# Stick-breaking attention of a streaming encoder layer: heads taken in pairs, the TensorE order written out

## The chip, the cores and the metric

One core of a Trainium2 chip runs the whole kernel in one launch. The metric is the time of one execution on the device in microseconds; the median of several runs is quoted. "The profile" is one execution taken by the hardware profiler, "the trace" its instructions.

## The reference

One layer of a hybrid encoder, for a prompt of 512 tokens and eight samples of 16 tokens each (640 token rows together), model width 1024, all in float32. After a norm, one wide input projection feeds three token mixers (stick-breaking attention, a pooling mixer, gated linear attention), whose outputs are gated, merged and projected; cross-attention into 256 memory tokens and a gated feed-forward block follow. The change is in the stick-breaking attention (6 heads of 64 channels):

```
z = einsum('bqhd,bkhd->bhqk', q, k) * 64 ** -0.5
mask = k_pos < q_pos
log_beta = log_sigmoid(z)
log_fail = where(mask, log_sigmoid(-z), 0)
after = cumsum(log_fail, axis=3, reverse=True) - log_fail
w = where(mask, exp(log_beta + after), 0)
out = einsum('bhqk,bkhd->bqhd', w, v)
```

Prompt queries see the prompt's own keys. Each sample's 16 queries see 256 cached keys and the sample's own 16.

## The kernel before

All weights are split into a high and a low part, and every large product is three matmuls per tile of 128 (`products`, L114). Weights arrive on SP's DMA queue in a ring of buffers (`raw`, three; `wh` and `wl`, four each): `load_raw` (L73), then a cast on ScalarE (L83) and a subtraction on VectorE (L89). The part of the input projection that is kept by rows comes in seven column blocks, n0 to n6, of five units each, one per 128 token rows (`nat_unit`); a unit is 24 matmuls into a PSUM bank with the tag g, and a ScalarE copy. Blocks 0 and 1 are done first. `proj_nat(2)` to `proj_nat(4)` stand in the program behind the attention, blocks 5 and 6 in the next stage (gated linear attention).

PSUM has eight banks, two for each of the tags g, t, z and o (`bank`, L63).

**Order.** Instructions are written as a plain program. The framework orders each engine's instructions by priority (place in the program) among those whose inputs and buffers are free, so work that stands later may run earlier. Inside `tc.manual_schedule(engines={PE})` TensorE's instructions keep the written order.

**What comes ahead of the attention.** Queries and keys are projected with channels on partitions into `qkT` (tiles 0 to 2 queries, 3 to 5 keys; of each tile, head 2p lies in rows 0 to 63, head 2p+1 in rows 64 to 127). Then five key blocks are transposed back (`tp_k`, L460), copied into `kst` (two buffers, L462) and stored (L464, L467). The pool `poolw`, which holds `kst` and the pooling mixer's tiles, is released, and the attention's pool `sbw` opens in its place.

**Attention.** A prompt unit is one query block i of 128 rows and one to three heads; with i + 1 key blocks its scores are at most 512 columns wide. `sb_prompt_a` makes the scores (`z`, L508, one head's 64 rows of the array), then `softplus` (Abs, Exp, Ln on ScalarE, L476 to L478; one VectorE instruction, L479), a mask on the diagonal block on GpSimd (L217), and `stick`: a scan from the right on VectorE (L487), `z` minus the scan (L488), Exp on ScalarE (L489), and a mask again. `sb_prompt_b` transposes the weights block by block (`tp_w`, L521), copies them out (L523) and, once both heads of a pair are there, multiplies with the values (`po`, L534, the two heads into the two halves of the output's partitions). A sample unit is a pair of heads and four samples: cached keys and values are loaded (`kn`, L544; `vn`, L548; one buffer each), keys are transposed (`tp_kc`, L555) and copied into `kt` (L556, L557), scores of four samples go to four groups of 32 output rows (`zs`, L567), then the same steps, 272 columns wide; `sb_sample_b` transposes (L582, L583), multiplies (`pos`, L587, L591), copies (L593), transposes back (L595) and splits. There are 18 prompt units (12 of one head with i = 3 and 2, 4 with i = 1, 2 of three heads with i = 0) and six sample units, one behind every three prompt units; `sb_..._b` of a unit stands two units behind its `sb_..._a`.

Of the kernel before, what the change touches and what calls it, by code (L numbers as in the profile page):

```python
# [16 lines left out]
P = 128  # L17
# [16 lines left out]
def tile_hybrid_stream_step(  # L34
# [466 lines left out]
    def sb_prompt_a(i, hs):  # L501

        n = (i + 1) * P
        m = len(hs)
        z = bank([P, 512], "z", "z")[:, 0:m * n]
        for j, h in enumerate(hs):
            p_, r = h // 2, slice((h % 2) * 64, (h % 2) * 64 + 64)
            nc.tensor.matmul(z[:, j * n:(j + 1) * n], qkT[r, p_, i * P:(i + 1) * P], qkT[r, 3 + p_, 0:n],  # L508
                             start=True, stop=True)
        t = softplus(z, m * n)  # L510
        mask_diag(t, i, m, n)
        w = stick(z, t, m, n)
        mask_diag(w, i, m, n)
        return w

    def sb_prompt_b(i, hs, w):
        n = (i + 1) * P
        m = len(hs)
        tp = bank([P, 512], "t", "tp_w")
        for k in range(m * (i + 1)):  # L520
            nc.tensor.transpose(tp[:, k * P:(k + 1) * P], w[:, k * P:(k + 1) * P], ident)  # L521
        wT = sbw.tile([P, 512], F32, tag="wT", bufs=2, name="wT")
        nc.vector.tensor_copy(wT[:, 0:m * n], tp[:, 0:m * n])  # L523
        for j, h in enumerate(hs):
            wTs[i, h] = wT[:, j * n:(j + 1) * n]
        if hs[0] == 0:
            oacc[i] = bank([P, 3, P], "o", "po")
        for h in hs:
            if h % 2 == 0:
                continue  # L530
            p_ = h // 2
            for k in range(i + 1):
                for r in range(2):
                    nc.tensor.matmul(oacc[i][64 * r:64 * r + 64, p_, :], va[:, k, (2 * p_ + r) * 64:(2 * p_ + r + 1) * 64],  # L534
                                     wTs[i, 2 * p_ + r][:, k * P:(k + 1) * P], start=(k == 0), stop=(k == i))
            if h == 5:
                split(oa_h[:, :, i * P:(i + 1) * P], oa_l[:, :, i * P:(i + 1) * P], oacc[i])

    def sb_sample_a(p_, g):
        kn = sbw.tile([P, 4, 2, P], F32, tag="kn", bufs=1, name="kn")  # L540
        vn = sbw.tile([P, 4, 2, P], F32, tag="vn", bufs=1, name="vn")
        for j in range(4):
            b = 4 * g + j
            nc.sync.dma_start(kn[:, j], cache_sb_k[0, b, :, 2 * p_:2 * p_ + 2, :]  # L544
                              .rearrange("(t p) h d -> p t (h d)", p=P))
        for j in range(4):
            b = 4 * g + j
            nc.sync.dma_start(vn[:, j], cache_sb_v[0, b, :, 2 * p_:2 * p_ + 2, :]  # L548
                              .rearrange("(t p) h d -> p t (h d)", p=P))
        kt = sbw.tile([P, 4, 272], F32, tag="kt", bufs=1, name="kt")  # L550
        for half in range(2):
            tp = bank([P, 2, 2, P], "t", "tp_kc")
            for j in range(2):
                for t_ in range(2):
                    nc.tensor.transpose(tp[:, j, t_, :], kn[:, 2 * half + j, t_, :], ident)  # L555
            nc.any.tensor_copy(kt[:, 2 * half:2 * half + 2, 0:256], tp.rearrange("p j t k -> p j (t k)"))  # L556
        nc.gpsimd.tensor_copy(kt[:, :, 256:272],  # L557
                              qkT[:, 3 + p_, 512 + 64 * g:576 + 64 * g].rearrange("p (j q) -> p j q", q=16))
        bdq = sbw.tile([P, 4, 32], F32, tag="bdq", bufs=2, name="bdq")
        nc.gpsimd.memset(bdq, 0.0)  # L560
        for r in range(2):
            rs = slice(64 * r, 64 * r + 64)
            nc.gpsimd.tensor_copy(bdq[rs, :, 16 * r:16 * r + 16],
                                  qkT[rs, p_, 512 + 64 * g:576 + 64 * g].rearrange("p (j q) -> p j q", q=16))
        z = bank([P, 272], "z", "zs")
        for j in range(4):
            nc.tensor.matmul(z[32 * j:32 * j + 32, :], bdq[:, j, :], kt[:, j, :],  # L567
                             start=True, stop=True)
        t = softplus(z, 272)
        nc.vector.tensor_tensor(t[:, 256:272], t[:, 256:272], smask, ALU.mult)  # L570
        w = stick(z, t, 1, 272)
        nc.vector.copy_predicated(w[:, 256:272], invm.bitcast(U32), zero16)
        we = sbw.tile([P, NB, 16], F32, tag="we", bufs=2, name="we")
        nc.vector.tensor_tensor(we, w[:, None, 256:272].broadcast_to([P, NB, 16]),
                                gmask[:, g, :, None].broadcast_to([P, NB, 16]), ALU.mult)
        return vn, w, we

    def sb_sample_b(p_, g, st):
        vn, w, we = st
        tp = bank([P, 3, P], "t", "tp_ws")  # L580
        for k in range(2):
            nc.tensor.transpose(tp[:, k, :], w[:, k * P:(k + 1) * P], ident)  # L582
        nc.tensor.transpose(tp[:, 2, :], we.rearrange("p b k -> p (b k)"), ident)  # L583
        wT = sbw.tile([P, 3, P], F32, tag="wT", bufs=2, name="wTs")
        nc.any.tensor_copy(wT, tp)
        po = bank([P, P], "o", "pos")
        nc.tensor.matmul(po, wT[:, 2, :], va[:, 4, p_ * P:(p_ + 1) * P], start=True, stop=False)  # L587
        for k in range(2):
            for j in range(4):
                js = slice(32 * j, 32 * j + 32)  # L590
                nc.tensor.matmul(po[js, :], wT[:, k, js], vn[:, j, k, :], start=False, stop=(k == 1))  # L591
        on = sbw.tile([P, P], F32, tag="on", bufs=1, name="on")
        nc.vector.tensor_copy(on, po)  # L593
        po = bank([P, P], "t", "tp_on")
        nc.tensor.transpose(po, on, ident)  # L595
        pv = po.rearrange("p (j r q) -> p j r q", r=2, q=16)
        for r in range(2):
            rs = slice(64 * r, 64 * r + 64)
            cs = slice(512 + 64 * g, 576 + 64 * g)
            split(oa_h[rs, p_, cs].rearrange("p (j q) -> p j q", q=16),  # L600
                  oa_l[rs, p_, cs].rearrange("p (j q) -> p j q", q=16), pv[rs, :, r, :])
# [4 lines left out]
    nc.gpsimd.memset(zero16, 0.0)  # L606

    up = [(3, (h,)) for h in range(6)] + [(2, (h,)) for h in range(6)]
    up += [(1, (0, 2)), (1, (1, 3)), (1, (4,)), (1, (5,)), (0, (0, 2, 4)), (0, (1, 3, 5))]
    us = [(p_, g) for p_ in range(3) for g in range(2)]  # L610
    units = []
    for j, u in enumerate(up):
        units.append((sb_prompt_a, sb_prompt_b, u))
        if j % 3 == 2 or j >= 17:
            if us:
                units.append((sb_sample_a, sb_sample_b, us.pop(0)))
# [869 lines left out]
```

## Time and profile before

| | |
|---|---|
| runs shown, median (lowest to highest) | 1299.34 us (1299.01 to 1300.34) |
| profiled execution, its own time | 1298.68 us |
| its span, first to last instruction | 1297.0 us |
| TensorE matmuls busy | 1275.6 us, 98% of the span |
| VectorE, ScalarE, GpSimd busy | 776.2, 596.5, 41.2 us |
| mean granted clock of TensorE | 0.997 of full speed |

The profile counts an engine as busy from an instruction's start to its end. Matmuls overlap each other, so what a matmul costs is read from start to next start. In a timeline row "x16" merges sixteen instructions, and the length runs from the first start to the last end. "z<-qkT 64x512" means that tile `z` is computed from tile `qkT`, 64 partitions by 512 elements; a float32 product of two operands appears as two matmuls, a transpose as one. A row's square bracket says how long the engine stood idle before it and what ended that. SP's queue shows when a DMA is issued, not when its data lands.

### The profile page before, as it was taken

How to read it: one execution, taken by the hardware profiler on the slowest of the kernel's cores; microseconds unless marked ns; L12 is line 12 of the kernel's file. 1: busy time of each engine (PE TensorE's matmuls, PEld its weight loads, DVE VectorE, ACT ScalarE, POOL GpSimd, SP SyncE). 2: the span in 40 equal slices, each digit the busy share in tenths (PEclk: the TensorE clock that was granted, in tenths of full speed). 3: DMA queues.
4: the chain of work that ended last, by engine and by line, in shares of the span. 5: the costliest groups of instructions: out<-in, count | busy, mean ns of one | idle time of the engine just before them, and what ended most of it. 6: DMA issues, size and time to landing. Idle time of an engine off the chain costs nothing.

```text
span 1297.0 us, 21377 instructions
## 1 busy us (share of the span) xinstructions
PE 1275.6 (98%) x8493; PEld 1156.5 (89%) x8493; DVE 776.2 (60%) x1458; ACT 596.5 (46%) x1198; POOL 41.2 (3%) x162
## 2 busy tenths in 40 slices
PE   8999999999999999999999999999999999999997
PEld 8998777988999999987998878899898989898995
DVE  7433875387478455437535434598466767675766
ACT  5324665454353445435434543476352525243452
POOL 2101111001000000000000000000000000000000
PEclk9999999999999999999999999999999999999999
DMA  7324332201321232232448860242232313132232
GB/s 239 103 78 120 94 100 66 62 1 55 82 78 32 82 122 67 72 143 69 133 178 273 299 224 1 81 147 82 65 98 76 98 54 114 49 98 82 82 123 105
DMA packets 132889, 133.88 MB, mean 103 GB/s; under 512 B 15798, under 2 KB 116741, under 8 KB 132789
## 3 DMA queue, kind: packets, MB, share of 16 engines
q1 hardware_dynamic: 132501, 132.23, 32.4%
q8 instruction: 67, 1.10, 0.3%
q0 software_dynamic: 288, 0.29, 0.1%
q14 instruction: 33, 0.27, 0.1%
HBM read 121.72 MB, written 10.77 MB: 102 GB/s over the span
## 4 chain that ended last, share of the span: by engine, by line
PE 91%; DVE 4%; ACT 2%; DMA 2%; issue 1%; SPq 0%; POOL 0%; DVEq 0%; ACTq 0%
PE ps_g L114 13%; PE fX L1237 11%; PE ps_d L114 8%; PE ps_n L114 8%; PE fZ L1237 5%; PE ps_xq L114 4%; PE ps_b L114 4%; PE acc L1308 4%; PE acc L1309 4%; PE acc L1310 3%; PE ps_qk L114 3%; PE fY L1237 3%; PE pl L721 2%; PE ps_xk L114 2%; PE ps_xv L114 1%; PE z L508 1%
## 5 line engine op out<-in xcount | busy, mean ns | idle before, releaser
L1308 PE MATMUL acc<-wh_o,ga_h 128*128 128x512 f32 (+1 forms) x224 | 87.4, 390 | 0.0
L1309 PE MATMUL acc<-wl_o,ga_h 128*128 128x512 f32 (+1 forms) x224 | 87.3, 390 | 0.0
L1310 PE MATMUL acc<-wh_o,ga_l 128*128 128x512 f32 (+1 forms) x224 | 87.2, 389 | 0.0
L816 ACT ACTIVATE sgm<-ps_g 128x320 f32<-128x320 f32 x48 | 20.9, 435 | 66.0 <-PE ps_g L114 65.9
L1310 PEld LDWEIGHTS acc<-wh_o,ga_l 128*128 128x128 f32 x224 | 42.0, 188 | 9.6
L1308 PEld LDWEIGHTS acc<-wh_o,ga_h 128*128 128x128 f32 x224 | 42.0, 188 | 9.3
L1309 PEld LDWEIGHTS acc<-wl_o,ga_h 128*128 128x128 f32 x224 | 42.1, 188 | 9.2
L1237 PE MATMUL fX<-fT_h,wl_f 128*128 128x320 f32 x160 | 49.5, 309 | 0.0
L1237 PE MATMUL fX<-fT_l,wh_f 128*128 128x320 f32 x160 | 49.4, 309 | 0.0
L1237 PE MATMUL fZ<-S_h,wl_f 128*128 128x320 f32 x160 | 49.4, 309 | 0.0
L1237 PE MATMUL fX<-fT_h,wh_f 128*128 128x320 f32 x160 | 49.4, 309 | 0.0
L1237 PE MATMUL fX<-S_h,wh_f 128*128 128x320 f32 x160 | 49.4, 309 | 0.0
L1237 PE MATMUL fX<-S_l,wh_f 128*128 128x320 f32 x160 | 49.4, 309 | 0.0
L1237 PE MATMUL fZ<-S_l,wh_f 128*128 128x320 f32 x160 | 49.4, 309 | 0.0
L1237 PE MATMUL fZ<-S_h,wh_f 128*128 128x320 f32 x160 | 49.4, 309 | 0.0
L1237 PE MATMUL fX<-S_h,wl_f 128*128 128x320 f32 x160 | 49.3, 308 | 0.0
L143 ACT CAST wh_f<-ra 128x1024 fp32r<-128x1024 f32 x20 | 21.0, 1052 | 45.9 <-PE acc L1310 26.8
L144 DVE TENSOR_TENSOR wl_f<-ta,wh_f 128x1024 fp32r<-128x1024 f32 x20 | 24.5, 1225 | 27.5 <-ACT wh_f L143 27.5
L817 DVE TENSOR_SCALAR sgm<-sgm 128x320 f32<-128x320 f32 x48 | 15.5, 325 | 40.4 <-ACT sgm L816 40.3
L143 ACT CAST wh_f<-ta 128x1024 fp32r<-128x1024 f32 x20 | 21.0, 1049 | 38.9 <-PE acc L1310 29.1
L1393 DVE TENSOR_TENSOR X<-acc,X 128x512 f32<-128x512 f32 x40 | 27.2, 690 | 17.9 <-PE acc L1310 17.9
L144 DVE TENSOR_TENSOR wl_f<-ra,wh_f 128x1024 fp32r<-128x1024 f32 x20 | 24.4, 1222 | 22.4 <-ACT wh_f L143 22.2
(1004 smaller groups left out, 4246.0 us busy)
## 6 DMA issues: line engine op xcount, KB each, us to landing
raw_o<-in_w_ffn_out_dram SPq DMA_DIRECT2D x22, 512.0 KB, 3.5
ra<-in_w_ffn_in_dram SPq DMA_DIRECT2D x40, 256.0 KB, 3.3
rb<-in_w_ffn_in_dram SPq DMA_DIRECT2D x40, 256.0 KB, 3.4
kc<-in_cache_mem_k_dram SPq DMA_DIRECT2D x16, 512.0 KB, 4.8
vc<-in_cache_mem_v_dram SPq DMA_DIRECT2D x16, 512.0 KB, 5.4
raw_mix<-in_w_mix_out_dram SPq DMA_DIRECT2D x8, 512.0 KB, 4.4
raw_xo<-in_w_xo_dram SPq DMA_DIRECT2D x8, 512.0 KB, 6.1
kn<-in_cache_sb_k_dram SPq DMA_DIRECT2D x24, 128.0 KB, 2.4
```

Of the source, the lines that this page charges most:

```text
L114: ins = nc.tensor.matmul(ps, a, b, start=(j == 0), stop=(j == len(todo) - 1))
L143: nc.scalar.copy(h, src)
L144: nc.vector.tensor_tensor(l, src, h.bitcast(F32), ALU.subtract)
L508: nc.tensor.matmul(z[:, j * n:(j + 1) * n], qkT[r, p_, i * P:(i + 1) * P], qkT[r, 3 + p_, 0:n], start=True, stop=True)
L721: nc.tensor.matmul(pl[0:nk, h], X[:, h, 0:nk], mv_, start=True, stop=True)
L816: nc.scalar.activation(s, ps, AF.Exp, scale=-1.0)
L817: nc.vector.tensor_scalar(s, s, 2.0 ** 63, None, ALU.min)
L1237: nc.tensor.matmul(ps, w_, m_, start=(start and j == 0), stop=(stop and j == 11), skip_group_check=True)
L1308: nc.tensor.matmul(ps, ah, wh[:, 0, c0:c0 + w], start=first, stop=False)
L1309: nc.tensor.matmul(ps, ah, wl[:, 0, c0:c0 + w], start=False, stop=False)
L1310: nc.tensor.matmul(ps, al, wh[:, 0, c0:c0 + w], start=False, stop=last)
L1393: nc.vector.tensor_tensor(dst, ps, dst, addop)
```

## The change

Prompt units become objects of an even and an odd head (or lists of them), sample units objects with their steps as methods, and TensorE's order over all of them and over the fifteen units of projection blocks 2 to 4 is written out. A prompt unit's `scores` issues the matmuls of the even and of the odd head in turn, into two z banks; `turn` transposes and copies the even head's weights on VectorE, the odd head's on ScalarE. There are now nine prompt units (three with i = 3, three with i = 2, two with i = 1, one with i = 0), with a sample unit behind each of the first six. A sample unit's `load` and `keys` stand right behind the scores of the sample unit before it; its output and the transpose back use g banks instead of o and t, the copies of `kt` go one to VectorE and one to ScalarE, `on` to ScalarE. In step j of the loop, TensorE does the transposes of unit j-2, the transpose back of unit j-3, one projection unit, the output of unit j-2, the scores of unit j, and the keys of the next sample unit. The first steps are the keys of sample unit 0 and the scores of prompt unit 0. `softplus`, `stick`, `mask_diag` and the sample unit's scores are the same as before. Cut to its core:

```diff
-    def sb_prompt_a(i, hs):
...
-        for j, h in enumerate(hs):
-            p_, r = h // 2, slice((h % 2) * 64, (h % 2) * 64 + 64)
-            nc.tensor.matmul(z[:, j * n:(j + 1) * n], qkT[r, p_, i * P:(i + 1) * P], qkT[r, 3 + p_, 0:n],
-                             start=True, stop=True)
...
+        def scores(self):
+            i, n = self.i, self.n
+            m = len(self.hs[0])
+            zs = [bank([P, 512], "z", "z")[:, 0:m * n] for _ in range(2)]
+            for j in range(m):
                 for r in range(2):
+                    p_, rs = self.hs[r][j] // 2, slice(64 * r, 64 * r + 64)
+                    nc.tensor.matmul(zs[r][:, j * n:(j + 1) * n], qkT[rs, p_, i * P:(i + 1) * P],
+                                     qkT[rs, 3 + p_, 0:n], start=True, stop=True)
+            self.w = []
+            for z in zs:
+                t = softplus(z, m * n)
+                mask_diag(t, i, m, n)
+                w = stick(z, t, m, n)
+                mask_diag(w, i, m, n)
+                self.w.append(w)
...
+                if r:
+                    nc.scalar.copy(wT[:, 0:len(hs) * self.n], tp[:, 0:len(hs) * self.n])
+                else:
+                    nc.vector.tensor_copy(wT[:, 0:len(hs) * self.n], tp[:, 0:len(hs) * self.n])
...
-            nc.any.tensor_copy(kt[:, 2 * half:2 * half + 2, 0:256], tp.rearrange("p j t k -> p j (t k)"))
...
+                if half:
+                    nc.scalar.copy(kt[:, 2:4, 0:256], tp.rearrange("p j t k -> p j (t k)"))
+                else:
+                    nc.vector.tensor_copy(kt[:, 0:2, 0:256], tp.rearrange("p j t k -> p j (t k)"))
...
-        po = bank([P, P], "o", "pos")
...
+            po = bank([P, P], "g", "pos")
...
-        nc.vector.tensor_copy(on, po)
-        po = bank([P, P], "t", "tp_on")
...
+            nc.scalar.copy(self.on, po)
...
-    up = [(3, (h,)) for h in range(6)] + [(2, (h,)) for h in range(6)]
-    up += [(1, (0, 2)), (1, (1, 3)), (1, (4,)), (1, (5,)), (0, (0, 2, 4)), (0, (1, 3, 5))]
...
-    for fb_, u_, st_ in pend:
-        fb_(*u_, st_)
-    for c in range(2, 5):
-        proj_nat(c)
+    pu = [PromptUnit(i, (h,), (h + 1,)) for i in (3, 2) for h in (0, 2, 4)]
+    pu += [PromptUnit(1, (0, 2), (1, 3)), PromptUnit(1, (4,), (5,)), PromptUnit(0, (0, 2, 4), (1, 3, 5))]
+    su = [SampleUnit(p_, g) for p_ in range(3) for g in range(2)]
     units = []
+    for j in range(len(pu)):
+        units.append(pu[j])
+        if j < len(su):
+            units.append(su[j])
+    fill = [(c, i) for c in range(2, 5) for i in range(NT)]
+    ws = {}
+    su[0].load()
+    with tc.manual_schedule(engines={mybir.EngineType.PE}):
+        su[0].keys()
+        units[0].scores()
+        for j in range(1, len(units) + 2):
+            old = units[j - 2] if 2 <= j else None
+            if old:
+                old.turn()
+            if 3 <= j and isinstance(units[j - 3], SampleUnit):
+                units[j - 3].back()
+            if fill:
+                c, i = fill.pop(0)
+                if i == 0:
+                    ws[c] = load_nat(c)
+                nat_unit(c, ws[c], i)
+            if old:
+                old.out()
+            if j < len(units):
+                units[j].scores()
+                if isinstance(units[j], SampleUnit):
+                    k = su.index(units[j]) + 1
+                    if k < len(su):
+                        su[k].load()
+                        su[k].keys()
```

## Rows read from the trace of the kernel before

**Rows 1.** The page: busy time by engine.
```profile
PE 1275.6 (98%) x8493; PEld 1156.5 (89%) x8493; DVE 776.2 (60%) x1458; ACT 596.5 (46%) x1198; POOL 41.2 (3%) x162
```

**Rows 2.** Busy time by stretch of attention: us, then PE, PEld, DVE, ACT, POOL, clock, DMA.
```profile
107.38:124.41 17.03, 16.97 (x121) 15.06 (x120) 6.37 (x9) 6.77 (x16) 2.83 (x9) 1.00 0.65 187
124.41:217.06 92.65, 91.54 (x684) 66.33 (x685) 69.96 (x137) 61.55 (x138) 15.92 (x52) 1.00 0.29 82
```

**Rows 3.** Timeline of two heads that start together: ScalarE, VectorE, GpSimd.
```profile
117.33 1.09 ACT L476 ACTIVATE sp<-z 128x512 f32<-128x512 f32 x2
...
120.00 1.29 DVE L479 SCALAR_TENSOR_TENSOR sp<-z,sp 128x512 f32<-128x512 f32 x2 [10.55 <-ACT sp L478]
121.21 2.56 DVE L487 TENSOR_TENSOR_SCAN w<-sp 128x512 f32<-128x512 f32 x2
123.69 1.26 DVE L488 TENSOR_TENSOR w<-z,w 128x512 f32<-128x512 f32 x2
...
125.68 0.29 POOL L217 TENSOR_SCALAR_AFFINE_SELECT w<-w 128x128 f32<-128x128 f32 x1 [0.31 <-ACT w L489]
```

**Rows 4.** Timeline of TensorE: first matmul of projection block 5.
```profile
217.06 0.29 PE L114 MATMUL ps_n<-wh_n5a,hT_h 128*128 128x278 f32 x1
```

**Rows 5.** Timeline of TensorE in attention: start, length (us), line, tile, how many.
```profile
107.38 1.12 PE L508 MATMUL z<-qkT 64*128 64x512 f32 x2
108.43 0.87 PE L460 MATMUL tp_k<-ident,qkT 128*128 128x128 f32 x6
...
116.84 0.29 PE L114 MATMUL ps_n<-wh_n2a,hT_h 128*128 128x276 f32 x1
...
119.89 0.29 PE L114 MATMUL ps_n<-wh_n2a,hT_h 128*128 128x276 f32 x1
...
139.24 0.49 PE L587 MATMUL pos<-va,wTs 128*128 128x128 f32 x2
139.66 0.65 PE L591 MATMUL pos<-vn,wTs 128*32 128x128 f32 x16
140.24 0.40 PE L114 MATMUL ps_n<-wl_n3a,hT_h 128*128 128x276 f32 x1
...
147.09 1.14 PE L567 MATMUL zs<-kt,bdq 128*32 128x272 f32 x8
148.16 0.65 PE L521 MATMUL tp_w<-ident,w 128*128 128x128 f32 x4
148.74 0.91 PE L508 MATMUL z<-qkT 64*128 64x384 f32 x2
149.58 0.66 PE L521 MATMUL tp_w<-ident,w 128*128 128x128 f32 x4
...
151.61 1.09 PE L534 MATMUL po<-wT,va 128*64 128x128 f32 x14
152.63 0.40 PE L114 MATMUL ps_n<-wh_n3a,hT_h 128*128 128x276 f32 x1
...
189.01 0.70 PE L508 MATMUL z<-qkT 64*128 64x256 f32 x2
```

**Rows 6.** Timeline of SP's queue (issues), and how long the key loads take.
```profile
111.38 1.10 SPq L464 DMA_DIRECT2D out_dram<-kst  x2
116.99 0.33 SPq L467 DMA_DIRECT2D out_dram<-kst  x1
117.80 1.98 SPq L544 DMA_DIRECT2D kn<-in_cache_sb_k_dram  x4
...
DMA to landing us min/median/max: 2.0/2.4/3.6
```

**Rows 7.** The same table of stretches, near the kernel's start.
```profile
10.00:11.00 1.00, 0.00 (x0) 0.00 (x0) 1.00 (x3) 0.00 (x0) 0.00 (x0) 1.00 1.00 325
11.00:12.00 1.00, 0.91 (x5) 0.94 (x6) 1.00 (x2) 0.00 (x0) 0.00 (x0) 0.75 1.17 282
...
14.00:15.00 1.00, 1.00 (x7) 1.00 (x6) 0.93 (x3) 1.00 (x1) 0.00 (x0) 0.55 1.17 339
```

More of the change, by code (lines that the diff above doesn't have):

```diff
@@ L499, in mask_diag @@
             sel(d, [[0, m], [-1, P]], 0, 1, ALU.is_gt)
-    def sb_prompt_a(i, hs):
-        n = (i + 1) * P
-        m = len(hs)
-        z = bank([P, 512], "z", "z")[:, 0:m * n]
-        for j, h in enumerate(hs):
-            p_, r = h // 2, slice((h % 2) * 64, (h % 2) * 64 + 64)
-            nc.tensor.matmul(z[:, j * n:(j + 1) * n], qkT[r, p_, i * P:(i + 1) * P], qkT[r, 3 + p_, 0:n],
-                             start=True, stop=True)
[L510 to L532, printed above, removed]
-                for r in range(2):
-                    nc.tensor.matmul(oacc[i][64 * r:64 * r + 64, p_, :], va[:, k, (2 * p_ + r) * 64:(2 * p_ + r + 1) * 64],
-                                     wTs[i, 2 * p_ + r][:, k * P:(k + 1) * P], start=(k == 0), stop=(k == i))
-            if h == 5:
-                split(oa_h[:, :, i * P:(i + 1) * P], oa_l[:, :, i * P:(i + 1) * P], oacc[i])
@@ L539, in sb_sample_a @@
[L539 to L555, printed above, removed]
-            nc.any.tensor_copy(kt[:, 2 * half:2 * half + 2, 0:256], tp.rearrange("p j t k -> p j (t k)"))
[L557 to L576, printed above, removed]
@@ new lines, in tile_hybrid_stream_step, with __init__, turn, out @@
+    class PromptUnit:
+        def __init__(self, i, ev, od):
+            self.i, self.n, self.hs = i, (i + 1) * P, (ev, od)
+        def scores(self):
[3 more added lines that the diff above has]
+            for j in range(m):
+                for r in range(2):
+                    p_, rs = self.hs[r][j] // 2, slice(64 * r, 64 * r + 64)
[8 more added lines that the diff above has]
+                self.w.append(w)
+        def turn(self):
+            for r, w in enumerate(self.w):
+                hs = self.hs[r]
+                tp = bank([P, 512], "t", "tp_w")
+                for k in range(len(hs) * (self.i + 1)):
+                    nc.tensor.transpose(tp[:, k * P:(k + 1) * P], w[:, k * P:(k + 1) * P], ident)
+                wT = sbw.tile([P, 512], F32, tag="wT", bufs=2, name="wT")
+                if r:
+                    nc.scalar.copy(wT[:, 0:len(hs) * self.n], tp[:, 0:len(hs) * self.n])
+                else:
+                    nc.vector.tensor_copy(wT[:, 0:len(hs) * self.n], tp[:, 0:len(hs) * self.n])
+                for j, h in enumerate(hs):
+                    wTs[self.i, h] = wT[:, j * self.n:(j + 1) * self.n]
+        def out(self):
+            i = self.i
+            if self.hs[0][0] == 0:
+                oacc[i] = bank([P, 3, P], "o", "po")
+            for h in self.hs[0]:
+                p_ = h // 2
+                for k in range(i + 1):
+                    for r in range(2):
+                        nc.tensor.matmul(oacc[i][64 * r:64 * r + 64, p_, :], va[:, k, (h + r) * 64:(h + r + 1) * 64],
+                                         wTs[i, h + r][:, k * P:(k + 1) * P], start=(k == 0), stop=(k == i))
+            if self.hs[1][-1] == 5:
+                split(oa_h[:, :, i * P:(i + 1) * P], oa_l[:, :, i * P:(i + 1) * P], oacc[i])
```

93 lines of the change are left out of this document (60 added, 33 removed).

## The prediction

> **What bounds the kernel now.** I read the page first: TensorE is busy for 98% of the span, VectorE, the next, for 60% [rows 1]. So a change pays only where it takes TensorE time away without making TensorE wait. The change touches one stage, from the first score matmul (107.38 us) to the end of attention. The table by stretches shows no hole there: TensorE is busy for 16.97 of 17.03 us and 91.54 of 92.65 us [rows 2]. The order in which instructions ran says why: whenever softplus, scan or exponential keep a head waiting, projection matmuls (`ps_n`, blocks 2 to 4 of the input projection) stand in. From 110 to 124 us TensorE ran little else, since softplus started only at 117.33 [rows 3]. What can be gained is therefore matmul time and the price of jumping between kinds of matmul; what can be lost is this cover.
>
> The stretch to 217.06, where a projection block of the next stage first appears [rows 4], is 109.7 us. The last sample unit still has 1.6 us to run then (the prices are below), and nine key transposes (`tp_k`) that stay take about 1.2 (six last 0.87). Attention with its fifteen projection units thus costs TensorE **110.1 us** now.
>
> **TensorE's work after the change**, from start to next start [rows 5]:
> - Fifteen projection units, each in one piece: 24 matmuls take 116.84 to 119.89, 3.05 us, and the first after another kind of matmul takes 0.40 instead of 0.29, so 3.16 each: 47.4. Before, these units were cut into pieces by other work, and that price was paid many times over.
> - Scores of prompt heads. A 512-column head alone takes 1.05 (two passes), a 384-column one 0.84, a 256-column one 0.70. Now two heads stand back to back in rows 0 to 63 and 64 to 127, into two PSUM banks. The trace before has no such pair. Bounds: they run together (a pair costs one head) or in turn (two). The nearest rows are the column groups: sixteen `pos` matmuls in four groups take 0.58, fourteen `po` in two groups 1.02, while six transposes of the same 128 columns last 0.87: 0.04 and 0.07 each against 0.14. I take "together", since the groups there overlap without being asked to. Four units of 512 columns, four of 384, one of 256: 8.3 (16.6 in turn).
> - Transposes of weights: 60 blocks, 0.58 for four with their switch: 8.7. Output matmuls: 120, 1.02 for fourteen: 8.7.
> - Six sample units: scores 1.07, output 0.42 + 0.58, three transposes 0.44, one back 0.2, eight key transposes 1.16: 3.87 each, 23.2.
>
> Sum 96.3, so TensorE's work falls by **13.8 us**, 8.3 of it the pairing, the rest fewer switches.
>
> **What the written order adds: the start.** The block begins with `keys` of the first sample unit, and nothing inside it, no projection unit either, may go ahead. Those transposes need the cached keys. Their load is a tile of the pool `sbw`, which opens where `poolw` is released, and before the change the load sits on SP's queue directly behind the last store of `kst` (116.99), at 117.80, although SP had nothing else to issue from 112.5 on [rows 6]. That store waits for a chain of copies and stores through two `kst` buffers; the change edits none of this. So I keep 117.80, four issues in 1.98 us, landing 2.4 after issue: the first half of the keys is there at about 121.0. Until then TensorE has only the `tp_k`. Work on projection block 5 cannot stand in: its weights need ring slots that blocks 2 and 3 hold. Loss 121.0 - 107.4 - 1.2 = **12.4 us**. Bounds: none if the load goes ahead of the last store; 13.6 if landing takes the 3.6 of its slowest.
>
> **What it adds: the score banks.** Scores have two PSUM banks (tag z). A prompt unit now takes both; the sample unit behind it needs the first again, free once `w = z - w` (L488) has read it. The nearest row is the very case: two 512-column heads that became ready together. Their softplus steps alternate on ScalarE; the first Abs starts at 117.33, the first L488 ends at 124.3: 7.0 us, 7.1 with the hop from TensorE [rows 3]. Meanwhile TensorE has, after the first unit, one projection unit (3.2), later a sample's three transposes, a projection unit and a sample's output (4.6). Waits: 3.9 after the first prompt unit, 2.5 after the second and third, 1.1 after the fourth and fifth (7.0 scaled by 0.84/1.05 is 5.6, 5.7 with the hop). After the sixth, block 5 has weights and stands in, as it does at the end before the change [rows 4]; so too for the last three prompt units, whose turn comes with little between. Sum **11.1**. Lower bound: the first head's steps go ahead of the second's. One head alone needs 0.6 three times, 0.65, 0.3 on GpSimd, 1.28 and 0.63, or 4.7 [rows 3], and only the first unit's bank waits (4.7 less 3.2, 1.5); but the second head's weights are ready no sooner than the row's 8.6 (125.68 + 0.29 - 117.33), which stops its transposes for some 1.5 in each of the three large units: 6 in all. Upper: 14, with a weight split of DVE or ScalarE in the way each time. I take 11.1, by the row nearest.
>
> **Edits that I cost at nothing.** The copies of `kt`, `on` and the odd head's `wT` change engine: ScalarE and VectorE are busy for 68 and 76 of 109.7 us there [rows 2], and a copy's consumer comes a projection unit later; without that cover each costs its 0.3 to 0.7. The value load of the next sample unit waits on SP for the output two units earlier; kept ahead of the next key load in the queue it would hold `keys` up by some 3 us five times. I take it that SP's order stays by readiness, as before. GpSimd's `kt` copy waits for the scores before it, with the prompt masks queued behind it, as now.
>
> **Sum.** -13.8 + 12.4 + 11.1 = +9.7 on the profiled execution's 1298.68 (span 1297.0 and 1.7 around it): 1308.4. That execution lies 0.66 below the median of the runs, 1299.34, so **1309.0**.
>
> **Rivals.**
> 1. *The first key load goes early* (faster). For: SP idles from 112.5, and of the old pool only `kst` is still in use. Against: it was idle before, too, and yet the load came behind the store. The 12.4 go to nothing, and -13.8 + 11.1 = -2.7 gives 1296.6. It turns the sign where the first `tp_kc` starts before about 111.3 us, when the start costs less than the 2.7 that are left.
> 2. *The first head runs ahead*, waits 6 instead of 11.1: 1303.9. For: matmuls leave in order. Against: the steps alternated in the row.
> 3. *The halves do not overlap*: +8.3, but the first head's scores are done half a pair earlier, which shortens the five waits by 4.8 in all: 1312.5. For: no row shows row halves at once. Against: the column groups. The Trainium skill (TensorE: Matmul & The Clock Gate, Part 3) says that matmuls in different row groups run at the same time; by that this rival would be out, and no run here shows it yet.
> 4. *The clock falls in the waits.* Between 10 and 11 us TensorE did nothing, and from 11 to 15 the granted clock was at its lower level, 1.2 GHz, for 3.4 us, which costs 1.7 [rows 7]. After the start gap I expect the same, hidden in the first bank wait, where TensorE has too little to do anyway. If it falls at four waits too: +6.8, 1315.8. Against: waits of 2.5 us are short beside the time at work. The Trainium skill (the same page, Part 1) says that the clock is taken back from an engine that stands idle; the row agrees for the one gap it has.
>
> **Chances.** Forecast 0.46; rival 1 0.18; rival 2 0.15; rival 3 0.10; rival 4 0.11. The range, **1296 to 1318**, leaves out nearly half of the first rival, a part of the fourth and the upper bounds of both waits together, some 0.2. A measurement of this kernel can tell 0.2%, 2.6 us, from no change. Faster by more (below 1296.7): over half of rival 1, and both waits near their lower bounds, 0.13. Within: the rest of rival 1 and the low end of rival 2, 0.12. Slower: 0.75.
>
> **What would show it.** After the change: a TensorE hole from about 112 to 121 us that ends with `tp_kc`, with the clock at its lower level behind it; `z` matmuls whose two heads start within nanoseconds, four in about 1.05 us; holes of 1 to 4 us ahead of `zs`, released by VectorE L488; projection units in unbroken runs of 24. I am wrong if `tp_kc` starts before 112, if `zs` finds its bank free, or if projection matmuls of blocks 2 to 4 run ahead of the first `keys`.

## The result, and the profile after

The changed kernel takes **1319.11 us** (median of four runs, 1316.72 to 1322.14), the one before, timed beside it, 1299.17 (1298.48 to 1300.34): ratio **1.015**, 95% interval 1.0128 to 1.0171. I had forecast 1309.0 and a range to 1318. Slower was right; the loss, 20 us, is twice what I gave. The profiled execution has a span of 1317.6 us against 1297.0, so 20.6 us are to be found in the trace.

The page of the changed kernel, busy time by engine (compare [rows 1]):

```profile
PE 1270.4 (96%) x8493; PEld 1159.2 (88%) x8493; DVE 773.8 (59%) x1449; ACT 598.0 (45%) x1207; POOL 43.3 (3%) x162
```

The table by stretches, columns as in [rows 2]; first the stretch from 107 us to the first key transpose of the next stage, then the parts of it (and one behind it) in which the granted clock is low:

```profile
107.00:238.90 131.90, 104.58 (x861) 84.43 (x859) 77.19 (x142) 72.54 (x170) 18.18 (x54) 0.91 0.30 86
107.00:125.00 18.00, 7.47 (x33) 4.05 (x31) 3.25 (x5) 4.06 (x8) 0.00 (x0) 0.62 0.69 198
...
131.00:135.00 4.00, 3.81 (x20) 3.37 (x20) 3.10 (x7) 2.54 (x6) 1.37 (x6) 0.57 0.27 77
...
215.00:224.00 9.00, 6.98 (x27) 5.67 (x28) 6.03 (x12) 4.36 (x11) 1.68 (x6) 0.62 0.01 2
...
312.00:323.00 11.00, 11.00 (x56) 11.00 (x55) 4.65 (x17) 3.62 (x8) 0.00 (x0) 0.53 0.00 0
```

The same stretch of the kernel before, up to the same transpose:

```profile
107.00:222.60 115.60, 114.43 (x861) 86.51 (x858) 80.06 (x151) 71.71 (x161) 18.75 (x61) 1.00 0.35 101
```

The reader sees two things. TensorE is busy for 9.9 us less than before (104.6 against 114.4), yet the stretch is 16.3 us longer, because it now stands idle for 27.3 us where it stood idle for 1.2. And the clock is at its lower level in four places where it was not before. Taking the table microsecond by microsecond, busy time times what the clock lacks of 1.00, TensorE lost 2.7, 1.6 and 3.1 us in the three places inside the stretch and 5.1 at 312. At full clock its work in the stretch is thus 97.1 us, 17.3 less than before. So the 16.3 are -17.3 (work), +26.1 (idle) and +7.4 (clock); the other 4.3 of the 20.6 come behind the stretch, where the fall at 312 costs 5.1.

Where the idle time is, from TensorE's timeline (start, length, line, tile, how many; in brackets the idle time before it and what ended it):

```profile
108.33 0.87 PE L460 MATMUL tp_k<-ident,qkT 128*128 128x128 f32 x6 [0.78 <-ACT kst L462]
111.27 0.90 PE L460 MATMUL tp_k<-ident,qkT 128*128 128x128 f32 x3 [2.06 <-ACT kst L462]
119.83 2.34 PE L572 MATMUL tp_kc<-ident,kn 128*128 128x128 f32 x8 [7.67 <-DMA kn<-in_cache_sb_k_dram]
122.10 2.08 PE L514 MATMUL z<-qkT 64*128 64x512 f32 x4
...
130.22 0.67 PE L589 MATMUL zs<-kt,bdq 128*32 128x272 f32 x8 [2.69 <-DVE w L488]
...
138.64 1.13 PE L514 MATMUL z<-qkT 64*128 64x512 f32 x4
...
145.70 0.67 PE L589 MATMUL zs<-kt,bdq 128*32 128x272 f32 x8 [1.61 <-DVE w L488]
146.30 1.09 PE L572 MATMUL tp_kc<-ident,kn 128*128 128x128 f32 x8
148.25 0.63 PE L529 MATMUL tp_w<-ident,w 128*128 128x128 f32 x4 [0.86 <-ACT w L489]
149.07 0.66 PE L529 MATMUL tp_w<-ident,w 128*128 128x128 f32 x4 [0.20 <-ACT kt L574]
...
216.88 2.51 PE L514 MATMUL z<-qkT 64*128 64x256 f32 x4 [2.45 <-DVE w L488]
...
235.16 0.55 PE L529 MATMUL tp_w<-ident,w 128*128 128x128 f32 x3 [1.34 <-POOL w L217]
```

The start has 10.5 us of holes (0.78, 2.06, 7.67). The sample scores wait for a score bank six times (2.69, 1.61 and 1.61, then 0.52, 0.52 and 0.58). The weight transposes `tp_w` wait 5.4 in all, 3.3 of it for the weights and 2.1 for `kt` on ScalarE: they need the PSUM bank that its copy empties. At the end stand 2.45 ahead of the scores of the eighth prompt unit and 1.34 ahead of the weights of the ninth. That is 27.2 of the 27.3. The four 512-column matmuls of a pair take 1.13 us at full clock (138.64), so the row halves do run together. `tp_kc` and the first `z` at half clock take 2.34 and 2.08 where the same ones later take 1.09 and 1.13.

SP's queue at the start (compare [rows 6]): the key load still stands behind the last store of `kst`.

```profile
116.55 0.33 SPq L467 DMA_DIRECT2D out_dram<-kst  x1
117.53 1.93 SPq L562 DMA_DIRECT2D kn<-in_cache_sb_k_dram  x4
```

### The profile page after: what moved, and what is told of

It reads as the page before. It is cut to its first block, busy times and chain, and to the rows that moved or that the text cites. A ratio compares the mean times of both kernels' runs of the same rounds, so it can differ in the third digit from the quotient of the medians.

```text
span 1317.6 us, 21366 instructions
## 1 busy us (share of the span) xinstructions
PE 1270.4 (96%) x8493; PEld 1159.2 (88%) x8493; DVE 773.8 (59%) x1449; ACT 598.0 (45%) x1207; POOL 43.3 (3%) x162
## 4 chain that ended last, share of the span: by engine, by line
PE 87%; DVE 6%; ACT 3%; DMA 2%; issue 1%; POOL 0%; SPq 0%; DVEq 0%; ACTq 0%; POOLq 0%
PE ps_g L114 13%; PE fX L1275 11%; PE ps_d L114 8%; PE ps_n L114 6%; PE fZ L1275 5%; PE ps_xq L114 4%; PE ps_b L114 4%; PE acc L1347 3%; PE acc L1346 3%; PE acc L1348 3%; PE fY L1275 3%; PE ps_qk L114 3%; PE pl L759 2%; PE ps_xk L114 2%; PE ps_xv L114 1%
## 5 line engine op out<-in xcount | busy, mean ns | idle before, releaser
L1431 DVE TENSOR_TENSOR X<-acc,X 128x512 f32<-128x512 f32 x40 | 27.2, 690 | 17.9 <-PE acc L1348 17.9
```

The source lines that it names most:

```text
L1431: nc.vector.tensor_tensor(dst, ps, dst, addop)
```

## The experiments

All ratios are to the kernel before on the same chip, with 95% intervals. "Next stage" is the start of the first matmul of branch a (`ps_b`), at 265.62 us in the profile of the kernel before and 282.15 in that of the changed one: up to there TensorE has the same work in all of them (1180 to 1187 matmul records from 107 us on; e4 has its added ones besides), so this column compares the attention stage. The last column is what TensorE lost to the lower clock in the profile, by the sum that gave 7.4 above, from 107 us to the next stage and behind it; the profile of the kernel before lost nothing there. A ratio comes from several executions, a profile is one. An edit is shown against the changed kernel unless another is named.

| kernel | ratio | interval | next stage, us | lost to the clock, us |
|---|---|---|---|---|
| changed | 1.0150 | 1.0128 to 1.0171 | 282.15 | 7.4, 5.1 |
| e12_after_again | 1.0139 | 1.0122 to 1.0156 | 281.58 | 5.5, 5.1 |
| e1_fill_ahead | 1.0046 | 1.0029 to 1.0063 | 273.45 | 3.4, 0 |
| e2_keys_other_queue | 1.0091 | 1.0062 to 1.0119 | 279.29 | 6.3, 1.7 |
| e3_zs_other_bank | 1.0293 | 1.0269 to 1.0316 | 306.20 | 20.7, 1.7 |
| e4_warm_start | 1.0148 | 1.0110 to 1.0187 | 284.62 | 7.9, 1.7 |
| e5_same_half | 1.0125 | 1.0108 to 1.0142 | 285.13 | 8.0, 1.7 |
| e6_zs_own_bank | 1.0160 | 1.0139 to 1.0181 | 288.18 | 11.7, 3.4 |
| e7_fill_before_turn | 1.0109 | 1.0090 to 1.0127 | 281.35 | 5.7, 0 |
| e8_ahead_block5 | 1.0001 | 0.9990 to 1.0013 | 269.55 | 5.1, 0 |
| e9_all | 1.0039 | 1.0020 to 1.0059 | 271.32 | 6.6, 3.4 |
| e10_split_fill | 1.0037 | 1.0020 to 1.0054 | 268.24 | 3.4, 3.4 |
| e13_wts_cover | 0.9983 | 0.9969 to 0.9997 | 261.95 | 1.7, 3.4 |
| e14 (e13, same half) | 0.9980 | 0.9967 to 0.9992 | 263.82 | 1.7, 0 |
| e15_back_later | **0.9919** | 0.9901 to 0.9937 | 258.45 | 1.7, 0 |
| e16 (e15, same half) | 0.9939 | 0.9917 to 0.9961 | 258.99 | 1.6, 3.4 |

### The start

```
-        su[0].keys()
         units[0].scores()
+        for _ in range(3):
+            c, i = fill.pop(0)
+            if i == 0:
+                ws[c] = load_nat(c)
+            nat_unit(c, ws[c], i)
+        su[0].keys()
```

> Edit: the first prompt scores and three projection units stand ahead of the first cached-key transposes; the rest of the order is as it was. Theory A (the 20 us are lost cover plus the lower clock that follows the holes): the start's holes of 10.5 us go to about 1, the first score-bank wait (2.7) goes, the clock stays at 1.00 from 107 to 135 us (4.3 us); against it the last three turns of the order lose their projection unit, up to 5 us of new waits there. About 1306, between 1300 and 1310. Theory B (the stage is now as long as the softplus and scan chains of ScalarE and VectorE, and a hole that is filled opens another further on): 1314 or more, with the score-bank and weight waits grown by what the start gave.

Table by stretches, and TensorE's waits (us in all, times, longest), of e1:

```profile
107.00:135.00 28.00, 26.09 (x189) 20.80 (x187) 13.07 (x21) 14.06 (x27) 2.85 (x8) 1.00 0.53 151
209.00:221.00 12.00, 8.31 (x52) 5.67 (x50) 8.76 (x17) 5.59 (x16) 2.92 (x7) 0.57 0.09 31
```
```profile
PE zs L589 <- DVE w L488: 5.0, 5, 1.8
...
PE z L514 <- DVE w L488: 3.6, 1, 3.6
```

In the first 28 us TensorE is idle for 1.9 and the clock holds at 1.00. Against 1.015 the ratio falls by 0.0104, 13.5 us, and the time is theory A's. The profile gives it less: the next stage starts 8.7 us earlier, where the theory's terms add up to 11.5 to 16.5, and the rest is the fall at 312, which is missing here and which the edit did not aim at. So the number was met in part by luck. The price came at the end: `z` now waits 3.6 us and the clock falls from 210 to 220.

```
-    su[0].load()
+    su[0].load(nc.gpsimd)
```

> Edit: the first key and value load is issued from GpSimd's queue instead of SP's, so that it does not stand behind the last store of kst; the order of TensorE is untouched. My step in the prediction (the first keys are late because of their place in SP's queue): the first tp_kc follows the tp_k at about 112 us, the hole of 7.7 us goes, the clock may still fall after the holes of 0.8 and 2.1 us between the tp_k: 1307 to 1312. Rival (the keys are held by their space, which comes free with the last kst copy, whichever queue issues them): first tp_kc at 118 or later, 1317 to 1321.

GpSimd issued the loads at 71.85 us. TensorE's timeline of e2:

```profile
111.81 0.55 PE L460 MATMUL tp_k<-ident,qkT 128*128 128x128 f32 x3 [2.34 <-ACT kst L462]
112.50 0.66 PE L572 MATMUL tp_kc<-ident,kn 128*128 128x128 f32 x4
117.96 1.11 PE L572 MATMUL tp_kc<-ident,kn 128*128 128x128 f32 x4 [4.80 <-ACT kst L462]
119.01 2.08 PE L514 MATMUL z<-qkT 64*128 64x512 f32 x4
```

The step of the prediction holds: from another queue the keys are there at once, and half of them are transposed at 112.50. But the other half waits until 117.96 for a bank, which the last `tp_k` holds until ScalarE can copy it into `kst`. The chain of `kst` copies that kept the load late on SP keeps the bank as well. By the ratios some 8 us came back, but the next stage starts only 2.9 us earlier; this profile, too, lacks the fall at 312.

```
+        dm = bank([P, 276], "o", "dm")
+        for k in range(63):
+            nc.tensor.matmul(dm, hT_h[:, k % KT, 0:P], hT_h[:, k % KT, 0:276], start=(k == 0), stop=(k == 62))
         su[0].keys()
```

> Edit: 63 matmuls whose result nobody reads stand ahead of the first cached-key transposes, about 8 us of the start's holes; nothing else is changed. Theory A (the lower clock behind the holes is a cost of its own): first tp_kc still at 119 to 121, but the granted clock stays at 1.00 from 107 to 135, which gives back 2.7 + 1.6 us: about 1315; if the fall at 312 us is a late echo of the start, another 5: 1310. Theory C (what ran at half clock behind the start is hidden in the first score-bank wait, as I wrote before): the wait ahead of the first zs grows by as much, 1318 to 1320.

The table by stretches of e4:

```profile
107.00:119.00 12.00, 9.99 (x78) 9.39 (x76) 2.63 (x4) 2.79 (x5) 0.00 (x0) 1.00 0.60 175
119.00:127.00 8.00, 5.85 (x19) 3.27 (x20) 0.69 (x1) 2.02 (x4) 0.00 (x0) 0.58 0.61 165
```

The clock held while the added matmuls ran, to 117.01. The keys came 1.1 us later than in the changed kernel (120.94), and in that hole of 3.9 the clock fell after all, so the first keys and scores ran at half clock here too. The experiment did not separate its theories.

### The score banks

```
-            z = bank([P, 272], "z", "zs")
+            z = bank([P, 272], "g", "zs")
```

> Edit: the sample units' scores take a bank of tag g instead of one of tag z. My step (sample scores wait for the bank of the prompt unit ahead): the waits of zs on VectorE L488, 7.5 us in all, go, and the rest stays: 1311 to 1313. Rival (the sample's steps then stand between those of the prompt heads on ScalarE and VectorE, and the weight transposes wait longer by as much): zs waits gone, tp_w waits up from 4 to about 10, 1316 to 1320.

TensorE's waits in e3, and its stretch from 107 to 265 us:

```profile
PE ps_n L114 <- DVE oa_l L144: 6.4, 3, 2.5
PE ps_n L114 <- DVE w L488: 3.6, 2, 2.4
```
```profile
107.00:265.00 158.00, 118.98 (x875) 98.13 (x874) 77.89 (x143) 74.42 (x173) 19.52 (x54) 0.82 0.26 75
```

Both theories missed, by 17 us and more. Tag g is the bank of the projection units: the very work that covers the holes now waits, 10 us in these two rows, for banks that sample scores and outputs hold. With holes in every turn the clock averages 0.82 over 158 us, and 13 of the 24 us by which the next stage starts later are lost to it.

```
+    po_all = bank([P, 3, P], "o", "po")
+    zs_all = bank([P, 272], "o", "zs")
-            z = bank([P, 272], "z", "zs")
+            z = zs_all
-                oacc[i] = bank([P, 3, P], "o", "po")
+                oacc[i] = po_all
```

> Edit: the sample units' scores have a PSUM bank of their own, the second of tag o; the prompt units' outputs share the first. Unlike tag g, tag o has no projection unit in it. My step (sample scores wait for the bank of the prompt unit ahead, 7.5 us in all): zs finds its bank free, and the kernel stands 12 to 14 us behind the one before instead of 20. Rival (the chains of ScalarE and VectorE set the pace, so the wait moves on to the weight transposes): zs waits gone, tp_w waits up from 4 to 10 us, 17 to 20 us behind.

TensorE's waits in e6:

```profile
PE tp_w L529 <- ACT w L489: 7.7, 7, 2.7
...
PE tp_w L529 <- ACT kt L574: 3.2, 4, 1.8
...
PE tp_w L529 <- DVE kt L576: 2.1, 1, 2.1
PE tp_w L529 <- POOL w L217: 1.9, 2, 1.3
```

The rival: no wait of `zs` is left, and `tp_w` waits 14.9 us in these rows instead of 6.7 in the changed kernel. The step "sample scores wait for the bank" was true, and taking it away was worth nothing, because the weights of the same prompt unit were late next. The next stage even starts 6.0 us later, 4.3 of it the clock.

```
-            if old:
-                old.turn()
-            if 3 <= j and isinstance(units[j - 3], SampleUnit):
-                units[j - 3].back()
             if fill:
...
                 nat_unit(c, ws[c], i)
-            if old:
-                old.out()
+            if old:
+                old.turn()
+            if 3 <= j and isinstance(units[j - 3], SampleUnit):
+                units[j - 3].back()
...
                         su[k].keys()
+            if old:
+                old.out()
```

> Edit: in each turn of the order the projection unit stands ahead of the weight transposes, and the output matmuls behind the next scores. Theory A (holes are a matter of what stands between a result and its use): the tp_w waits of 0.2 to 0.9 us, 4 us in all, go, since a projection unit is 3.2 us, and the zs waits shrink a little, by the output matmuls that now stand ahead of them: 14 to 17 us behind the kernel before instead of 20. Rival: no gain, since the zs waits take up what the tp_w waits give: 19 to 21 behind.

TensorE's waits in e7:

```profile
PE zs L589 <- DVE w L488: 8.7, 6, 2.8
PE z L514 <- DVE w L488: 4.2, 3, 2.4
...
PE tp_w L529 <- POOL w L217: 0.3, 1, 0.3
```

The time fits theory A, the trace doesn't: `tp_w` fell to 0.3, but `zs` and `z` rose to 12.9 together (10.0 in the changed kernel), and the next stage starts only 0.8 us earlier. The profile of e7 has no fall of the clock near 312; that is where its gain is. So within the stage the rival held.

### The two row halves

```
-                    p_, rs = self.hs[r][j] // 2, slice(64 * r, 64 * r + 64)
+                    p_, rs = self.hs[r][j] // 2, slice(0, 64)
```

> Edit: both heads of a pair read the queries and keys of rows 0 to 63, so that their score matmuls stand in the same row half; the odd heads' scores are then those of the even heads. If the halves do run together, as the pair of 1.06 us for four matmuls in the changed kernel says, a 512-column pair takes 2.1 us here, TensorE has 8.3 us more to do, and the zs waits shrink by at most what the first head is ahead, 5: 3 to 8 us slower than the changed kernel, 23 to 28 behind the kernel before. Rival (the halves never overlapped, the rows only look so): no difference in the pair's duration, 20 behind.

TensorE's timeline of e5, the second pair (in the changed kernel: 1.13):

```profile
140.62 1.98 PE L514 MATMUL z<-qkT 64*128 64x512 f32 x4
```

A pair in one half takes 1.98 us, so the overlap is real, as the Trainium skill has it (TensorE: Matmul & The Clock Gate, Part 3). It is worth less than the matmul time that it saves. Without it TensorE's busy time up to the next stage, counted at full clock, is 5.5 us more (145.7 against 140.2), but the bank waits of `zs` shrink from 7.5 to 2.0 us and the next stage starts only 3.0 us later. The kernel as a whole is no slower than the changed one (1.0125 against 1.0139 on the same chip), but that shows little of the halves: its profile lost 1.7 us to the clock behind the stage instead of 5.1.

### The clock

> No edit: the changed kernel once more, for the places where its clock falls. If the falls hang on the holes ahead of them, those at 110, 131 and 216 us come again, each behind a hole of 2 us or more, and the one at 312 us, with no hole of over 0.6 us ahead of it, need not. If it does come again in the same place, it belongs to the program.

The table by stretches of this second profile of the changed kernel:

```profile
107.00:125.00 18.00, 6.46 (x25) 2.90 (x22) 2.92 (x5) 2.97 (x6) 0.00 (x0) 0.59 0.65 187
131.00:135.00 4.00, 3.09 (x27) 2.21 (x28) 3.51 (x7) 2.85 (x7) 1.57 (x6) 1.00 0.23 65
...
312.00:321.00 9.00, 9.00 (x43) 9.00 (x43) 4.05 (x15) 2.35 (x6) 0.00 (x0) 0.50 0.00 0
```

The falls of the start and of the end (now 219 to 223) came again, behind holes of 8.3 and 2.45 us. The one at 131 did not (1.00), behind a hole of 1.7 instead of 2.7. The one at 312 did, in the same place, with no hole over 0.6 us in the 20 us ahead of it; by what I had written, it belongs to the program. But in the profiles of twelve of the fourteen other changed kernels, whose instructions on TensorE there are the same, it is missing, and in e3 and e4 it is shorter. What decides it stays open.

### Covering the holes

Beside e1's edit, e8 has

```
-    fill = [(c, i) for c in range(2, 5) for i in range(NT)]
+    fill = [(c, i) for c in range(2, 6) for i in range(NT)]
...
-            if fill:
+            for _ in range(2 if j in (13,) else 1):
+                if not fill:
+                    break
...
-    for c in range(5, 7):
-        proj_nat(c)
+    proj_nat(6)
```

> Edit: as e1_fill_ahead, and the five units of projection block 5 join the order, one in each of the last turns and two in the thirteenth. In e1 the end of the order had holes of 1.9 and 3.6 us and the lower clock from 210 to 220 us. Theory A: these go, and 5 to 9 us come back of the 6 that e1 stood behind the kernel before: between 3 us ahead of it and 2 us behind. Rival (the next stage needs block 5 as its own cover, which it now lacks): the holes move behind the order, 4 to 7 us behind.

Level with the kernel before, as theory A had it, though the next stage still starts 3.9 us later in the profile. Block 5 closed the end of the order.

Then e6, e7 and e8 together, in e9 as they are, with `range(2)` units ahead and `j in (13, 14)`:

> Edit: e6, e7 and e8 together, with two units ahead of the first keys instead of three and two units in the thirteenth and the fourteenth turn. Theory A: with the start, both kinds of wait and the end covered, the 17 us of TensorE work that the pairing and the fewer switches save come through, less some 3 to 6 us of holes and of lower clock that are left: 9 to 14 us ahead of the kernel before. Rival (chains of ScalarE and VectorE as the bound): 0 to 4 us ahead, with waits of tp_w on the weights of the turn before.

and in e10 with e2 as well and the loop in another form (shown against e9; `project` runs one unit of `fill`; what it is given runs behind the twelfth of its 24 matmuls):

```
+            if j in (13, 14):
+                project()
+            if isinstance(old, SampleUnit):
+                project(old.turn)
+            else:
+                project()
+                if old:
+                    old.turn()
             if j < len(units):
                 units[j].scores()
+            if old:
+                old.out()
+            if j < len(units) and isinstance(units[j], SampleUnit):
...
```

> Edit: the first keys from GpSimd's queue (e2), two units ahead of them, a bank of its own for zs (e6), block 5 in the order (e8), and in the turns where a sample's weights are transposed the projection unit is cut in two, one half ahead of the transposes and one behind, so that the copy of wTs has 1.6 us of cover; output matmuls stand ahead of the next keys. Theory A (each hole is one result with too little work between it and its use): no hole over 1 us between 115 and 200 us, hence no fall of the clock there, 8 to 14 us ahead of the kernel before. Rival (chains as the bound): 2 us ahead to 4 behind, with holes of 1 to 2 us at other places.

The longest of TensorE's waits in e9, and in e10:

```profile
PE tp_kc L572 <- DVE wTs L605: 6.1, 4, 2.1
```
```profile
PE pos L611 <- DVE wTs L607: 8.6, 5, 2.3
```

VectorE's timeline of e9, at one of these copies:

```profile
139.51 1.22 DVE L487 TENSOR_TENSOR_SCAN w<-sp 128x512 f32<-128x512 f32 x1
140.64 0.53 DVE L605 COPY wTs<-tp_ws 128x384 f32<-128x384 f32 x1
```

Both stand 0.4% behind the kernel before, behind what either theory gave, e9 by 5 us and e10 by 1. The clock has its part in that: it cost e9 6.6 us in the stage and each of them 3.4 behind it. The waits of `zs` for its bank and the `tp_w` waits are gone, but in e9 the next keys stand right behind the transposes of a sample's weights and wait for their copy `wTs` (their banks), and in e10 the output does (e9 also waits 4.0 for the first keys, which still come by SP's queue). The copy is short (0.53 us in e9), but VectorE takes it up only behind the scan of a prompt head (1.22 us) and what that scan waits for. That points to VectorE's order and not its load; the next kernel takes the point up. Against e10, e13 has

```
     su[0].load(nc.gpsimd)
+    su[0].prep()
...
-            if isinstance(old, SampleUnit):
-                project(old.turn)
+            if isinstance(old, SampleUnit) or j >= len(units):
+                old.turn()
+                project()
```

(`prep` holds the GpSimd instructions of `keys`.)

> Edit: as e10, but in a sample unit's turn the whole projection unit stands between the weight transposes and the output that needs their copy, the last two turns likewise, and the first sample's queries are set out by GpSimd ahead of the first masks. In e10 the five holes ahead of pos (2.3, 2.3, 1.3, 1.3, 1.3 us) and the one ahead of the first zs (3.3) were 12 of 16 us of holes. Theory A (cover): these fall to under 4 together, and the kernel is 4 to 9 us ahead of the one before. Rival (chains of ScalarE and VectorE): the holes come back at tp_w or zs, and it stands within 3 us of the kernel before.

The longest of TensorE's waits in e13:

```profile
PE tp_on L623 <- ACT on L619: 5.7, 5, 1.8
```

The `wTs` waits are gone, and the next stage starts 3.7 us before that of the kernel before. The gain in time is 2 us, under my 4 to 9, for two reasons: `tp_on` now waits 5.7 for its copy on ScalarE, and behind the stage the clock fell once, which cost 3.4. That fall is the clearest of all. In e13, and then in the kernel before, at the same hole ahead of `pl` (1.52 and 1.53 us long):

```profile
396.00:398.00 2.00, 0.50 (x5) 0.53 (x6) 2.00 (x7) 0.00 (x0) 0.00 (x0) 1.00 0.00 0
398.00:405.00 7.00, 6.99 (x32) 6.85 (x32) 4.79 (x14) 2.07 (x4) 0.00 (x0) 0.55 0.11 37
```
```profile
399.50:401.50 2.00, 0.53 (x6) 0.56 (x6) 2.00 (x7) 0.00 (x0) 0.00 (x0) 1.00 0.00 0
401.50:408.00 6.50, 6.49 (x49) 6.14 (x48) 5.78 (x17) 2.45 (x5) 0.41 (x1) 1.00 0.12 40
```

The same work, the same hole: once the clock went to its lower level for 7 us, once it stayed. All seventeen profiles have this hole, 1.52 or 1.53 us long: 7 us at the lower level follow it in e6, e9, e10, e13 and e16, half as much in e5, and none in the other eleven.

Against e13, e15 has

```
-            if 3 <= j and isinstance(units[j - 3], SampleUnit):
-                units[j - 3].back()
...
                 project()
+                if 3 <= j and isinstance(units[j - 3], SampleUnit):
+                    units[j - 3].back()
```

> Edit: e13 with the transpose back of a sample unit's output (tp_on) moved behind the next projection unit, so that the copy on ScalarE ahead of it has 3.2 us of cover. Theory A (cover): the tp_on waits, 5.7 us in e13, go to under 1, and the kernel is 4 to 8 us ahead of the one before. Rival (the chains): the holes come back at tp_w, z or po, less than 2 us gained on e13.

The longest of TensorE's waits in e15, and its stretch up to the next stage's first key transpose:

```profile
PE tp_w L529 <- POOL w L217: 2.0, 2, 1.3
```
```profile
107.00:227.70 120.70, 112.09 (x957) 95.38 (x955) 78.09 (x143) 72.64 (x175) 23.16 (x59) 0.99 0.31 88
```

No kind of wait is over 2.0 us in all, the clock averages 0.99, and the kernel takes 1292.10 us against 1301.96 of the kernel before on the same chip: **0.81% less**, and by the ratios 2.3% less than the changed one. That is more than theory A's 4 to 8 us; by the profiles the next stage starts 7.2 us earlier than in the kernel before. Of the 8 us that the ratios give it over e13, 3.5 are in the stage; e13's profile also lost 3.4 behind it, which e15's did not. e15 is the changed kernel with e2's queue, two units ahead of the keys, e6's banks, block 5 in the order, `prep`, and the loop as edited above. TensorE's idle time from 107 us to the next stage's first key transpose is 8.6 us instead of 27.3.

The last two kernels are e13 and e15 with e5's edit:

> Edit: e13 with both heads of a pair in the same row half, so that their scores run in turn; the odd heads' scores are then those of the even heads. If TensorE sets the time once the holes are covered, the 8.3 us of the pairing show nearly whole: 6 to 9 us slower than e13. If the chains still do, 0 to 3 us, as in e5.

> Edit: e15 with both heads of a pair in the same row half; the odd heads' scores are then those of the even heads. If TensorE sets the time in e15, 4 to 8 us slower than e15. If chains still set it, 0 to 3 us slower.

TensorE's score matmuls from 100 to 240 us, in e15 and in e16 (in e13 and e14 they are busy for the same 11.2 and 16.0):

```profile
L514 PE MATMUL z<-qkT 64*128 64x512 f32 (+3 forms) x48 | 11.2, 470 | 1.2 <-DVE w L488 1.2
L514 PE MATMUL z<-qkT 64*128 64x512 f32 (+3 forms) x48 | 16.0, 455 | 0.7 <-DVE w L488 0.7
```

e14 is level with e13, e16 2.6 us behind e15 by the medians of the ratios, with intervals that overlap. These times mix in the fall behind the stage, which e13's profile has and e14's does not, and which e16's has and e15's does not. In the stage e14 is behind by 1.9 us and e16 by 0.5, though their score matmuls take 4.8 us more: up to the next stage TensorE stands idle for 2.9 us less in each. Of what the overlap of the row halves saves TensorE, two fifths reach the end of the stage in the one pair of profiles and a tenth in the other.

## Why the prediction was right in sign and wrong in size

**TensorE's work.** I had -13.8; it is -17.3 at full clock. The direction and the reason (fewer switches, units in one piece) hold. Pairs cost what I took (at full clock 1.06 from start to next start with 512 columns), but two heads in one half would have cost less, 1.91 (e5) and not 2.1: the pairing's own share is 5.5 (e5), not 8.3, and the switches' is larger.

**The start.** I had 12.4; the holes are 10.5. The place of the key load in SP's queue was right, but it was not all that held the keys: with the load early, half of them still waited for a bank until 117.96 (e2). Right, too, was that nothing written behind the keys came ahead of them; written ahead of them it does (e1). The first rival, an early load, is out.

**The score banks.** I had 11.1; they are 7.5. The mechanism was right (VectorE L488 ends all six), but my 7.0 us of chain was too long: from the first Abs (124.21) to the end of the first L488 it is 5.9. In the row that I took it from both scans stood ahead of the first L488; here the first head's L488 goes ahead of the second head's scan:

```profile
129.39 0.68 DVE L488 TENSOR_TENSOR w<-z,w 128x512 f32<-128x512 f32 x1
129.99 1.22 DVE L487 TENSOR_TENSOR_SCAN w<-sp 128x512 f32<-128x512 f32 x1
```

The second rival named that direction.

**Costed at nothing, and not nothing.** Two covers failed. "A copy's consumer comes a projection unit later" looks at the consumer only: the bank that the copy empties is wanted at once, by `tp_w`, 2.1 us; and I had given no time to the weights themselves being late, 3.3 (e6 shows both grow). And "block 5 has weights and stands in" behind the sixth unit and the last three: nothing from outside the written order came in before block 5 started at 231.51, ahead of the last unit's weights, and the end has 3.8 us of holes. e8 put it there by hand.

**The clock: the step that failed.** I wrote that the lower clock behind the start gap is "hidden in the first bank wait" and gave falls at later waits 0.11, since waits of 2.5 us were "short beside the time at work". Neither holds. Behind the start it was the first keys and the first scores that ran at half clock, 2.2 us late together, and the bank wait only begins with those scores. Behind the holes of 2.69 and 2.45 us the clock fell again (in e12, behind the second and not behind a first one of 1.71), and once more at 312. In all TensorE lost 12.5 us. The fourth rival, at 1315.8, was nearest, and that in part by luck: it too has the two covers at nothing, 9.2 us, which nearly cancel against the terms that I had too high. The Trainium skill (TensorE: Matmul & The Clock Gate, Part 1) says that an idle engine loses its clock; the rows agree behind the start and behind holes of 2.69 and 2.45 us that I took for harmless, and do not explain the fall at 312, with no hole over 0.6 us ahead of it.

Together: 9.7 as forecast, +7.4 in the stage and +4.3 behind it, where the clock fell, +5.4 and +3.8 for the waits costed at nothing, -3.6 (banks), -1.9 (start), -3.5 (work) and -1.2 (idle before) make 20.4, against 20.6 measured.

**The third rival** (halves in turn) is out by the row of 1.13 us (1.98 in one half), but its price was the better lesson. I had added the pairing's saving and the waits as if they were separate terms. e5, e14 and e16 show that they trade: more than half of what TensorE saves in scores it stands idle for at the next waits (2.9 to 3.1 us of 4.8 to 5.5).

## What to carry to other kernels

When an order is written out by hand, list for each matmul not only its inputs but the bank it writes, and count the work between the last reader's start and that matmul; a copy that was free under a free order can become a hole, and closing one hole shows the next (bank, weights, `wTs`, `on` here). Judge such a change only when all are covered: the same units were 1.5% behind in the order given and 0.8% ahead with cover. Matmul time saved ahead of a wait for another engine was worth a tenth to a half of itself here, and holes cost more than their length, since the clock may fall behind them.

## What the runs showed of the hardware

The clock's fall is not a fixed price of a hole. The same hole of 1.5 us, ahead of the same work, was followed by 7 us at the lower level in five of seventeen profiles and by none in eleven (rows above); in e10 two holes of 2.32 us stand 16 us apart, at 138.2 and 154.5, and only the first was followed by a fall (142 to 145 us). What decides between them was not found.
